# A two-part weight stream in which every other mixing unit gets its low part by an adding transfer

## The chip, the cores and the metric

The kernel runs on one core of a Trainium2 chip. The metric is the device time of one execution in microseconds (us), the median over several runs. The engines are named as in the profile: PE is TensorE (its weight loads are PEld), DVE is VectorE, ACT is ScalarE, POOL is GpSimd, SP is SyncE.

## The reference

The kernel computes a two-layer encoder trunk on a sequence of 512 positions and 1024 channels, in float32. Cut to what matters here, each layer is:

```
h = rmsnorm(x, mix_norm[i])
z = h @ w_in[i]
u_rnn, u_gelu, c_q, ckv_rope, fq, fk, fv, f_logit, gate_logit = split_columns(z)
y_a = rglru_branch(u_rnn, u_gelu, ...) @ w_br_a[i]     # causal conv, gates, associative scan, times GeLU
y_b = mla_branch(c_q, ckv_rope, ...) @ w_br_b[i]       # attention over compressed keys and values
y_c = fox_branch(fq, fk, fv, f_logit, ...) @ w_br_c[i] # attention with cumulative forget gates
g = sigmoid(gate_logit + gate_b[i])
x = x + (g[0] * y_a + g[1] * y_b + g[2] * y_c) @ w_o[i]
x = x + swiglu(rmsnorm(x, ffn_norm[i]))
x = x + sigmoid(rmsnorm(x, ple_norm[i]) @ w_ple_gate[i]) * (p[i] @ w_ple[i])
```

A final RMSNorm follows. Everything up to `w_o` is called the mixing part.

## The kernel before, in words

**Two-part products.** A float32 value is split into a high part (the value cast to the type float32r) and a low part (the value minus the high part). A product of two such values takes three matmuls: high by high, high by low, low by high (`mm3`, whose matmuls are line L237). Activations are kept in pages `pr`, 1024 columns wide: the high part in the first 512, the low part in the rest. Plain float32 pages of 512 columns are `pf` (20 of them).

**The weight stream.** The host packs all weights, in the order of their use, into one DRAM tensor `wst` of 606 units; a unit is 128 partitions by 512 columns of float32, 256 KB, and holds four tiles of 128 columns. Units 0 to 302 belong to layer 0 and 303 to 605 to layer 1; in each layer roughly the first 150 are those of the mixing part. The class `Stream` brings a unit in three steps:

- `_load` (L99) loads it by SP's DMA queue into one of four slots of the tile `raw`.
- `_split` casts it on ACT into the high half of one of eight pages of the tile `hl` (L112), and subtracts on DVE, `raw` minus the high part, into the low half of the page (L113).
- `tile` and `wide` hand the parts to the matmuls. Before a unit u is first used, `_ensure` has written down the splits up to unit u + 7, and the loads up to four units beyond those.

A page of `hl` is free for unit u + 8 when the last matmul of unit u has read it, and a slot of `raw` is free for unit u + 4 when both the cast and the subtraction of unit u have read it. A normal unit feeds 12 matmuls; the four units in `PACKED` feed 8.

**The order of work.** The program is written in the order of the mathematics; the order of the instructions on each engine is then fixed when the kernel is built, by a planner that plays the program through with its own times (`TileContext(nc, schedule_with_timeline_sim=True)`). Instructions under `high_priority()`, which the cast and the subtraction are, go first among those that are ready. On the chip each engine works through its list in that order, and a DMA is issued in the list of the engine that it was given to.

**Around the recurrence.** In `mix` each layer runs in this order: the recurrence's inputs (`ev_u`: convolution on DVE, split into `xcp`), the rotary key and the forget logits (`key_and_forget`, with a chain of small operations on POOL, L376 to L379, a DMA at L527 and one at L534, and a scan on DVE at L537), the GeLU inputs (`ev_ug`), the first pair of keys and queries of the forgetting attention (`fox_proj(0, ...)`, casts at L566), then the gate products of the recurrence (`lru_gate`, four tiles, Tanh and Exp on ACT), then `lru_tail`: four square roots on ACT, and for each of four tiles on DVE two products, a scan (L666), a third product and a split. After it come the values (`values`) and `renorm`, which loads x again through POOL's queue (L695), eight tiles, scales each on DVE, and splits it into the pages `Xn`: the high part by ACT (L233), the low part by DVE. The attention then interleaves its scores with projections (`fp`) and merges (`mg`) that read `X`, `Xn` and the recurrence's result `yA`. The helpers `stt` (L218), `tt` (L221), `ts` (L225 and L227) and `act` (L230) each have one line, so the profile shows much of this under a helper's line. POOL's queue also carries the memsets and small DMAs of the attention heads (L587, L589, L594, L596) and the loads of tables (L495).

Of the kernel before, what the change touches and what calls it, by code (L numbers as in the profile page):

```python
# [10 lines left out]
F32 = mybir.dt.float32  # L11
F32R = mybir.dt.float32r
I32 = mybir.dt.int32
AF = mybir.ActivationFunctionType
ALU = mybir.AluOpType
# [22 lines left out]

NUNITS = 606
KEPT = NUNITS - 16  # L40
PACKED = (8, 9, 311, 312)


# [41 lines left out]
class Stream:  # L85
# [15 lines left out]
    def _split(self, u):  # L101
        s = (u % self.nraw) * 512
        src = self.raw[:, s:s + 512]
        if u >= KEPT:
            self.kept[u] = self.pages.take()
        hi, lo = self._parts(u)
        if u in PACKED:
            hi, lo = (x.rearrange("p (k c) -> p k c", c=128)[:, :, 64 * i:64 * i + 64]
                      for i, x in ((0, hi), (1, hi)))
            src = src.rearrange("p (k c) -> p k c", c=128)[:, :, 0:64]  # L110
        with self.tc.high_priority():
            self.nc.scalar.copy(hi, src)  # L112
            self.nc.vector.tensor_tensor(lo, src, hi.bitcast(F32), op=ALU.subtract)  # L113

    def _parts(self, u, c=slice(0, 512)):
        if u in self.kept:
# [5 lines left out]
    def _ensure(self, u):  # L122
        last = min(u + self.nhl - 1, max(u + 4, KEPT - 1), NUNITS - 1)
        while self.loaded < min(self.nraw, NUNITS):
            self._load(self.loaded)
            self.loaded += 1
        while self.done <= last:
            self._split(self.done)
            self.done += 1
            while self.loaded < min(self.done + self.nraw, NUNITS):  # L130
                self._load(self.loaded)
                self.loaded += 1
# [34 lines left out]
class Trunk:  # L167
# [273 lines left out]
    def mix(self, layer):  # L441
# [69 lines left out]
        def key_and_forget():  # L511
# [3 lines left out]
            for k, x in enumerate(X):  # L515
                assert self.w.pos // 4 in PACKED
                wh, _ = self.w.tile(("kf", L, k))
# [621 lines left out]
    def ple_last(self, X, pw):  # L1139

        L, st = DEPTH - 1, self.st
        self.w.align()
        assert self.w.pos == 4 * KEPT
        fin = [{}, {}]
        half = [slice(0, SEQ // 2), slice(SEQ // 2, SEQ)]

        def part(i, j):
            t = half[i]
            b = self.banks.take()
            for k in range(KD):  # L1150
                if i == 0:
                    wh, wl = self.w.tile(("w_ple_gate", L, 128 * j, 128, k))
                else:
                    wh, wl = self.w.again(4 * KEPT + KD * j + k)
                self.mm3(b[:, :SEQ // 2], wh, wl, X[k].h[:, t], X[k].l[:, t], k == 0, k == KD - 1)
# [236 lines left out]
```

## Time and profile before

| what | value |
|---|---|
| median of 3 runs | 1833.72 us (1833.48 to 1834.23) |
| the profiled execution | 1832.69 us |
| its span, first to last instruction | 1830.8 us |
| granted TensorE clock, mean | 0.992 |
| casts of units on ACT (L112, into `hl`) | 590, 364.2 us busy, 618 ns each |
| subtractions of units on DVE (L113, into `hl`) | 590, 404.6 us busy, 686 ns each |
| read from HBM | 173.98 MB |

The span in 40 equal slices, each digit the busy share of a slice in tenths (9 is 90% or more), PEclk the granted TensorE clock in tenths:

```
PE   9979999999999999999999899999999999999997
DVE  8896678866665555444778966888576655553446
ACT  5755556553333333223448556565533333332243
POOL 1130001100000000000102200010000000000000
PEclk9989999999999999999999999999999999999999
```

PE is full nearly everywhere; the third slice, and the 23rd (the same place in layer 1), are where it is not. The times of single instructions, waits and stretches come from the trace of the same execution; "idle before" or a bracket such as [1.39 <-DVE pr L221] gives how long an engine had been idle before an instruction, and what released it.

### The profile page before, as it was taken

The numbers are of one execution on the slowest core, as the hardware profiler recorded it, in microseconds if no ns is written. First come the engines' busy times: TensorE is split into PE (matmuls) and PEld (weight loads), VectorE is DVE, ScalarE is ACT, GpSimd is POOL, SyncE is SP. The second block draws the span as 40 slices with busy tenths as digits, with TensorE's granted clock in tenths as the row PEclk, the third lists the DMA queues.
The fourth block names the chain that finished last, engine by engine and source line by source line (L and its number), as shares of the span: only waits on it lengthen the run. The fifth ranks groups of instructions, "written<-read, shape, count | busy, mean of one in ns | idle before, by whom it ended". The sixth has DMA issues, their size and how long they took to land.

```text
span 1830.8 us, 24152 instructions
## 1 busy us (share of the span) xinstructions
PE 1805.4 (99%) x8476; PEld 1504.4 (82%) x8476; DVE 1210.4 (66%) x2421; ACT 817.5 (45%) x1562; POOL 117.2 (6%) x234
## 2 busy tenths in 40 slices
PE   9979999999999999999999899999999999999997
PEld 7858888888888888888888788888888888888887
DVE  8896678866665555444778966888576655553446
ACT  5755556553333333223448556565533333332243
POOL 1130001100000000000102200010000000000000
PEclk9989999999999999999999999999999999999999
DMA  6232223324322332322433322243242332233331
GB/s 205 88 117 81 82 81 116 97 71 133 98 93 97 98 98 97 108 95 98 132 111 116 105 85 78 89 121 88 81 131 94 98 97 94 97 110 98 98 98 47
DMA packets 98825, 184.17 MB, mean 101 GB/s; under 512 B 13552, under 2 KB 14752, under 8 KB 98704
## 3 DMA queue, kind: packets, MB, share of 16 engines
q1 hardware_dynamic: 89280, 162.04, 27.1%
q0 software_dynamic: 8416, 19.45, 3.9%
q8 instruction: 66, 1.08, 0.2%
q10 hardware_dynamic: 1008, 1.14, 0.2%
q14 instruction: 55, 0.45, 0.1%
HBM read 173.98 MB, written 4.21 MB: 97 GB/s over the span
## 4 chain that ended last, share of the span: by engine, by line
PE 95%; DVE 3%; ACT 1%; issue 1%; DVEq 0%; ACTq 0%
PE bank L237 93%; PE bank L830 2%; DVE pf L218 1%; DVE pr L221 1%; ACT pf L230 0%; DVE hl L113 0%; DVE pf L666 0%; ACT pr L566 0%; DVE pf L221 0%; DVE pr L218 0%; ACT hl L112 0%; DVE small L838 0%; DVE bank L221 0%; DVE small L218 0%; ACT L230 0%
## 5 line engine op out<-in xcount | busy, mean ns | idle before, releaser
L237 PE MATMUL bank<-pr,hl 128*128 128x512 f32 (+1 forms) x6812 | 1605.2, 392 | 10.6 <-DVE pr L221 5.5
L237 PEld LDWEIGHTS bank<-pr,hl 128*128 128x128 f32 (+1 forms) x6812 | 1269.7, 188 | 274.5 <-DVE pr L221 8.0
L112 ACT CAST hl<-raw 128x512 fp32r<-128x512 f32 x590 | 364.2, 618 | 654.0 <-PE bank L237 438.8
L113 DVE TENSOR_TENSOR hl<-raw,hl 128x512 fp32r<-128x512 f32 x590 | 404.6, 686 | 365.4 <-ACT hl L112 349.5
L221 DVE TENSOR_TENSOR pf<-pf 128x512 f32<-128x512 f32 (+3 forms) x235 | 151.2, 652 | 31.9 <-ACT pf L230 29.8
L221 DVE TENSOR_TENSOR pf<-bank,pf 128x512 f32<-128x512 f32 (+3 forms) x198 | 132.9, 676 | 56.8 <-PE bank L237 31.7
L230 ACT ACTIVATE pf<-pf 128x512 f32<-128x512 f32 (+1 forms) x145 | 86.0, 600 | 112.5 <-DVE pf L221 109.8
L237 PE MATMUL bank<-pr 128*128 128x256 f32 (+4 forms) x704 | 119.6, 301 | 4.1 <-ACT pf L230 4.1
L237 PEld LDWEIGHTS bank<-pr 128*128 128x128 f32 (+1 forms) x704 | 103.9, 191 | 14.5 <-ACT pf L230 4.4
L230 ACT ACTIVATE pf<-bank,small 128x128 f32<-128x128 f32 (+3 forms) x130 | 69.0, 532 | 45.8 <-DVE small L838 42.8
L221 DVE TENSOR_TENSOR pr<-pf,pr 128x512 fp32r<-128x512 f32 (+3 forms) x126 | 85.6, 683 | 4.7 <-ACT pr L233 3.1
L855 ACT CAST pth<-bank 128x128 fp32r<-128x128 f32 (+3 forms) x128 | 54.2, 426 | 69.7 <-PE bank L830 65.6
L233 ACT CAST pr<-pf 128x512 fp32r<-128x512 f32 (+2 forms) x114 | 70.3, 620 | 29.0 <-DVE pf L218 19.2
L838 DVE TENSOR_REDUCE small<-bank 128x1 f32<-128x128 f32 (+3 forms) x128 | 61.7, 485 | 19.2 <-PE bank L237 18.2
L221 DVE TENSOR_TENSOR ptl<-bank,pth 128x128 fp32r<-128x128 f32 (+3 forms) x128 | 61.7, 484 | 13.8 <-ACT pth L855 11.7
L237 PE MATMUL bank<-hl,pr 128*128 128x512 f32 x240 | 56.5, 390 | 0.0
L830 PE MATMUL bank<-identr,pf 128*128 128x128 f32 x320 | 55.4, 274 | 0.0
L237 PEld LDWEIGHTS bank<-hl,pr 128*128 128x128 f32 x240 | 44.9, 188 | 9.2
L225 DVE TENSOR_SCALAR pf<-pf,small 128x128 f32<-128x128 f32 (+3 forms) x128 | 48.3, 383 | 2.6
L218 DVE SCALAR_TENSOR_TENSOR pf<-pf,bank 128x512 f32<-128x512 f32 x48 | 32.7, 684 | 23.7 <-PE bank L237 23.3
L230 ACT ACTIVATE pf<-bank,vec 128x512 f32<-128x512 f32 x60 | 40.9, 689 | 15.1 <-PE bank L237 14.7
L830 PEld LDWEIGHTS bank<-identr,pf 128*128 128x128 f32 x320 | 39.8, 141 | 7.2
(112 smaller groups left out, 793.2 us busy)
## 6 DMA issues: line engine op xcount, KB each, us to landing
raw<-wst SPq DMA_DIRECT2D x606, 256.0 KB, 2.6
pf<-xT POOLq DMA_DIRECT2D x16, 256.0 KB, 3.1
pr<-pr POOLq DMA_DIRECT2D x32, 128.0 KB, 2.5
pf<-xs POOLq DMA_DIRECT2D x16, 256.0 KB, 3.1
pf<-trig POOLq DMA_DIRECT2D x12, 256.0 KB, 3.1
pf<-xT SPq DMA_DIRECT2D x8, 256.0 KB, 5.4
xs<-pf POOLq DMA_DIRECT2D x8, 256.0 KB, 2.8
pf<-pT POOLq DMA_DIRECT2D x4, 256.0 KB, 3.1
```

The costliest lines, as they stand in the source:

```text
L112: self.nc.scalar.copy(hi, src)
L113: self.nc.vector.tensor_tensor(lo, src, hi.bitcast(F32), op=ALU.subtract)
L218: self.nc.vector.scalar_tensor_tensor(out, a, s, b, op0=op0, op1=op1)
L221: self.nc.vector.tensor_tensor(out, a, b, op=op)
L225: self.nc.vector.tensor_scalar(out, a, s1, None, op0=op0)
L230: return self.nc.scalar.activation(out, a, f, **kw)
L233: self.nc.scalar.copy(hi, src)
L237: self.nc.tensor.matmul(out, a, b, start=start, stop=stop, skip_group_check=True)
L830: nc.tensor.transpose(T[:, c], p2.ap[:, c], self.ident[:, :])
L838: nc.vector.reduce_max(R[t][:, 0:1], S[:, :m], axis=AX.X, negate=True)
L855: self.nc.scalar.copy(hi, src)
```

## The change

For 120 units of the mixing part, the odd ones from 11 to 129 in layer 0 and from 315 to 433 in layer 1, the low part is made differently. ACT casts the unit as before (L112). Then ACT, too, writes the negated high part into the low half of the page, and a DMA in POOL's queue reads the same unit a second time from `wst` and adds it to what stands there. DVE's subtraction falls away for these units. The unit is still loaded into `raw` for the cast; that slot is now read by the cast alone. All of it stands under `high_priority()`.

```
+ADDED = {*range(11, 130, 2), *range(315, 434, 2)}
...
         with self.tc.high_priority():
             self.nc.scalar.copy(hi, src)
-            self.nc.vector.tensor_tensor(lo, src, hi.bitcast(F32), op=ALU.subtract)
+            if u in ADDED:
+
+                self.nc.scalar.activation(lo, hi.bitcast(F32), AF.Copy, scale=-1.0)
+                c = 512 * (u % 2)
+                self.nc.gpsimd.dma_start(lo, self.wdram[u // 2][:, c:c + 512], accum_op=ALU.add)
+            else:
+                self.nc.vector.tensor_tensor(lo, src, hi.bitcast(F32), op=ALU.subtract)
```

The order in which the recurrence and the first keys and queries stand is the same before and after. The plan of all engines is made anew for the changed program.

## Prediction

> **What bounds the kernel now.** I read the page first: the busy times and the chain of work that ended last.
>
> ```profile
> PE 1805.4 (99%) x8476; PEld 1504.4 (82%) x8476; DVE 1210.4 (66%) x2421; ACT 817.5 (45%) x1562; POOL 117.2 (6%) x234
> PE 95%; DVE 3%; ACT 1%; issue 1%; DVEq 0%; ACTq 0%
> ```
>
> TensorE (PE) is busy for 1805.4 of 1830.8 us, and 95% of the chain is its own. Taking work off VectorE (DVE) can pay only where DVE is what PE waits for. The 4% of the chain that lies on DVE and ScalarE (ACT) is in two places, one in each layer: around the end of the recurrence, where `lru_tail`, the value evacuations and `renorm` meet. The busy times by stretch show them (columns: stretch, its length, PE, PE weight loads, DVE, ACT, POOL with instruction counts, then granted clock, DMA share, GB/s):
>
> ```profile
> 67.00:90.00 23.00, 23.00 (x104) 19.03 (x103) 16.36 (x29) 22.55 (x37) 8.06 (x18) 1.00 0.31 103
> 90.00:108.00 18.00, 18.00 (x83) 15.01 (x82) 17.91 (x26) 8.88 (x16) 4.74 (x9) 1.00 0.33 104
> 108.00:128.00 20.00, 9.99 (x28) 5.76 (x27) 19.87 (x40) 13.71 (x25) 10.58 (x21) 0.72 0.46 147
> 128.00:132.00 4.00, 4.00 (x14) 3.15 (x13) 4.00 (x10) 1.85 (x5) 0.00 (x0) 0.69 0.16 59
> 972.00:996.00 24.00, 24.00 (x108) 19.88 (x107) 16.08 (x27) 23.75 (x39) 11.21 (x24) 1.00 0.28 88
> 996.00:1020.00 24.00, 24.00 (x110) 19.89 (x109) 24.00 (x39) 14.81 (x26) 8.90 (x18) 1.00 0.49 155
> 1020.00:1028.00 8.00, 3.33 (x11) 1.95 (x10) 7.91 (x15) 5.11 (x11) 3.35 (x7) 0.80 0.34 100
> 1028.00:1032.00 4.00, 4.00 (x11) 3.01 (x11) 4.00 (x11) 1.39 (x3) 0.00 (x0) 0.55 0.32 111
> ```
>
> The same sequence runs in both layers. First ACT is full (22.55 of 23 us; 23.75 of 24) while PE runs on. Then DVE is full for 38 and 32 us, and at the end of that PE starves: it idles 10.0 us in 108 to 128 and 4.7 us in 1020 to 1028, and comes back at a lowered clock (0.69 and 0.55 in the next 4 us). So at most some 15 us of idle time and a few us of slow clock can be won. What ends both stalls, in the timeline of PE:
>
> ```profile
> 127.48 2.93 PE L237 MATMUL bank<-pr,hl 128*128 128x512 f32 x6 [1.39 <-DVE pr L221]
> 1024.57 1.05 PE L237 MATMUL bank<-pr,hl 128*128 128x512 f32 x2 [1.90 <-DVE pr L221]
> 1027.13 5.10 PE L237 MATMUL bank<-pr,hl 128*128 128x512 f32 x12 [1.51 <-DVE pr L221]
> ```
>
> A subtraction that writes a page of split activations (`pr`) releases it, which stands at the end of DVE's queue of work. Every instruction that DVE need not do ahead of it brings PE back earlier.
>
> **Part one: the subtractions that go.** Which units of the stream fall into a stretch comes from counting L113 (and L112) from the start; the n-th is unit n-1:
>
> ```profile
> L113 DVE TENSOR_TENSOR hl<-raw,hl x36: 406/675/730, 6.0 to 85.5; 128x512 fp32r<-128x512 f32 x34, 128x256 fp32r<-128x256 f32 x2
> L113 DVE TENSOR_TENSOR hl<-raw,hl x46: 406/681/730, 6.0 to 123.8; 128x512 fp32r<-128x512 f32 x44, 128x256 fp32r<-128x256 f32 x2
> L113 DVE TENSOR_TENSOR hl<-raw,hl x338: 406/691/730, 6.0 to 991.2; 128x512 fp32r<-128x512 f32 x167, 128x256 fp32r<-128x256 f32 x2
> L113 DVE TENSOR_TENSOR hl<-raw,hl x347: 406/691/730, 6.0 to 1022.6; 128x512 fp32r<-128x512 f32 x172, 128x256 fp32r<-128x256 f32 x2
> ```
>
> These are the counts up to 91.0, 127.4, 995.9 and 1026.9 us. Units 36 to 45 are subtracted in the full stretch of layer 0, units 338 to 346 in that of layer 1. The odd ones are in `ADDED`: five (37 to 45) and four (339 to 345). What one is worth is its pitch, not its duration, since neighbours overlap:
>
> ```profile
> 108.75 0.68 DVE L113 TENSOR_TENSOR hl<-raw,hl 128x512 fp32r<-128x512 f32 x1
> 109.35 0.68 DVE L221 TENSOR_TENSOR pr<-pf,pr 128x512 fp32r<-128x512 f32 x1
> ```
>
> 0.60 us each: 5 x 0.60 = 3.0 us in layer 0 and 4 x 0.60 = 2.4 us in layer 1. The other 111 of the 120 I cost at nothing: PE is busy 99% of the span, and outside the two stalls its own queue of matmuls is the cover. Were that cover gone, each would be worth up to 0.60 us.
>
> **Part two: what ACT gets.** Each added unit costs ACT one more 128x512 instruction, the negation. It doesn't occur in the trace; the nearest rows are the cast with its pitch and the plain activations:
>
> ```profile
> 81.78 0.62 ACT L112 CAST hl<-raw 128x512 fp32r<-128x512 f32 x1
> 82.29 0.83 ACT L230 ACTIVATE pf<-pf,msp 128x512 f32<-128x512 f32 x1
> L230 ACT ACTIVATE pf<-pf 128x512 f32<-128x512 f32 (+1 forms) x145 | 86.0, 600 | 112.5 <-DVE pf L221 109.8
> ```
>
> Between 0.51 us (the cast's pitch) and 0.60 us (the activation's mean); I take 0.55, nearer to the cast, whose types and queue it shares. It matters where ACT is full, before the square roots on which `lru_tail` waits:
>
> ```profile
> L112 ACT CAST hl<-raw x31: 405/622/626, 4.6 to 69.7; 128x512 fp32r<-128x512 f32 x29, 128x256 fp32r<-128x256 f32 x2
> L112 ACT CAST hl<-raw x36: 405/622/626, 4.6 to 84.2; 128x512 fp32r<-128x512 f32 x34, 128x256 fp32r<-128x256 f32 x2
> L112 ACT CAST hl<-raw x332: 405/622/632, 4.6 to 970.8; 128x512 fp32r<-128x512 f32 x164, 128x256 fp32r<-128x256 f32 x2
> L112 ACT CAST hl<-raw x338: 405/622/632, 4.6 to 990.6; 128x512 fp32r<-128x512 f32 x167, 128x256 fp32r<-128x256 f32 x2
> 87.59 1.34 ACT L230 ACTIVATE pf<-pf,eps 128x512 f32<-128x512 f32 x2
> 89.26 1.22 DVE L537 TENSOR_TENSOR_SCAN pf<-one,pf 8x512 f32<-8x512 f32 x1 [3.03 <-DMA pf<-pf]
> 90.50 1.29 DVE L218 SCALAR_TENSOR_TENSOR pf<-pf 128x512 f32<-128x512 f32 x2
> 992.48 1.95 ACT L230 ACTIVATE pf<-pf,eps 128x512 f32<-128x512 f32 x3
> 993.23 1.31 DVE L218 SCALAR_TENSOR_TENSOR pf<-pf 128x512 f32<-128x512 f32 x2 [1.34 <-ACT pf L230]
> ```
>
> The counts are up to 79, 87.5, 974 and 991.1 us: units 31 to 35 and 332 to 337 are cast there, three odd ones each time, so the roots come 3 x 0.55 = 1.65 us later. In layer 1 DVE waits for them (1.34 us, released by ACT), so its full stretch starts 1.65 us later. In layer 0 it doesn't: DVE's tail starts at 90.50, behind the scan of the forget gates, while the first root is done at about 88.3. Shifted by 1.65 that is 89.9, still ahead of 90.50. If the scan itself comes a little earlier, the tail starts 0.5 us earlier; I count those 0.5 us. The scan hangs on a chain of small operations on POOL that starts at 76.46, behind a wait for DVE:
>
> ```profile
> 76.46 0.31 POOL L376 TENSOR_SCALAR pf<-pf 128x32 f32<-128x32 f32 x1 [30.66 <-DVE pf L221]
> ```
>
> Ten subtractions (odd units 11 to 29) are gone from DVE before that point; if only three of them still show there, their 1.8 us pay for the three transfers (units 31 to 35) that now stand in this chain at 0.54 us each.
>
> **Part three: the adding transfers.** Issue and landing of an accumulating transfer aren't in the trace. The nearest are plain 256 KB loads on POOL's queue, one of them issued while DVE is full, and the load on SyncE's queue:
>
> ```profile
> 110.33 0.54 POOL L695 DMA_DIRECT2D pf<-xT  x1 [0.69 <-DVE pr L221]
> pf<-xT POOLq DMA_DIRECT2D x16, 256.0 KB, 3.1
> raw<-wst SPq DMA_DIRECT2D x606, 256.0 KB, 2.6
> q0 software_dynamic: 8416, 19.45, 3.9%
> ```
>
> From below 0.54 us of POOL and 3.1 us to landing; from above twice the landing, 6.2 us, since the old contents have to be read too. I take 4.5 us, between them for want of a nearer row; nothing in the sum depends on it while the lead covers it. The lead is shortest around unit 31:
>
> ```profile
> 79.59 0.61 ACT L112 CAST hl<-raw 128x512 fp32r<-128x512 f32 x1
> 0.00:89.70 89.70, 83.11 (x364) 68.01 (x365) 23.88 (x36) 22.51 (x37) 1.00 0.45 150
> ```
>
> The second row counts instructions on `hl` alone: 364 matmuls are the 31 units 0 to 30 (29 of 12 and two packed ones of 8), so PE reaches unit 31 at 89.70, 10.1 us after its cast began. Cast, negation and transfer take 0.5 + 0.55 + 4.5 = 5.6 us, at most 7.3. Bandwidth is no bound: q0 moved 19.45 MB in 3.9% of the 16 engines' time; 31.5 MB more are 6.3%, or 12.6% if each byte counts twice, on top of 0.46 to 0.49 in the stretches. What the transfer frees is small: an odd unit's `raw` slot comes free after the cast instead of the subtraction.
>
> The Trainium skill, "SBUF — State Buffer", section "SBUF: two separate sides", speaks against the change: while DVE runs an instruction that takes both its ports, GpSimd can't write descriptors, and a 620 ns transfer was seen to take 3100 ns. By it each transfer in a full stretch would, as an estimate, hold POOL about 2.5 us longer, and rival C would be the likeliest. The trace doesn't show it: the load at 110.33 was issued in 0.54 us in a stretch where DVE worked 19.87 of 20 us.
>
> **The sum.** Layer 0: -3.0 - 0.5 = -3.5 us. Layer 1: -2.4 + 1.65 = -0.75 us. Together -4.25 us. The profiled execution took 1832.69 us (span 1830.8 and 1.9 around it), 1.03 us under the median of 1833.72; from 1832.69 it goes to 1828.4, from the median to 1829.5. A change of 0.2%, 3.7 us, is about what a measurement of this kernel can tell from none.
>
> **The rivals.**
> A, the forecast: 1829.5; by itself 1827.8 (without the 1.65 us delay of layer 1's roots) to 1830 (without the 0.5 us).
> B, ACT gives it back: the scan doesn't come earlier, the roots come late in layer 0 too (-3.0 + 1.65 = -1.35), layer 1 as above: -2.1 us, 1831.6. For it: ACT is full ahead of both stretches. Against: the scan, not the roots, opens layer 0's.
> C, slower: POOL's queue becomes the bound. It runs in order (30.66 us of waiting at L376 show it), so an adding transfer whose negation is late holds the `renorm` loads behind it, and Xn comes late.
>
> ```profile
> 119.61 0.56 POOL L695 DMA_DIRECT2D pf<-xT  x1 [2.26 <-DVE pr L221]
> 126.09 0.73 DVE L218 SCALAR_TENSOR_TENSOR pf<-pf,vec 128x512 f32<-128x512 f32 x1
> ```
>
> The last load is issued at 119.61, lands about 122.7 and is used by 126.09 at the latest: 3.4 us of slack. Past that it decides. Five transfers at 0.54 us use 2.7 of it; if each also waits 1 us for ACT (one or two instructions of 0.6), it is 7.7 - 3.4 = +4.3 us, nothing is won by the subtractions, and in layer 1 about the same: +8.6, 1842.3. For it: POOL is busy 10.58 of 20 us there. Against: the casts run far ahead of PE.
> D, more is won: layer 1's stall closes altogether, because DVE's earlier relief (odd units from 315) also reaches ACT. That is 4.7 us idle and 4.0 x (1 - 0.55) = 1.8 us of slow clock; with layer 0's 3.5 us, -10 us, 1823.7. The clock fell to 0.55 after waits of 1.90 and 1.51 us at most.
> The Trainium skill, "TensorE: Matmul & The Clock Gate", section "HAM oscillation — how this bites in real kernels", wants idle gaps over about 3.4 us for that. By its rule the 1.8 us couldn't be lost in layer 1, and D would give 1825.5; the measured clock decides here.
>
> **How the numbers follow.** A 0.42, B 0.25, C 0.21, D 0.12. Faster by over 0.2% (under 1830.1): A and D, 0.54. Within 0.2%: B, 0.25. Slower (over 1837.4): C, 0.21. The range 1823 to 1841 holds A, B and D and the milder part of C; what is left out is C's centre and a transfer that is slow in itself. A's own range is 1827.8 to 1830.
>
> **What would show it right or wrong.** Right: 120 instances of L113 fewer, 120 more ACT instructions of about 0.6 us and 120 transfers of 256 KB on POOL; PE's idle time in layer 0's stretch down from 10.0 to about 6.5 us; layer 1's roots about 1.65 us later against the matmuls. Wrong: PE waiting on a DMA into `hl`; POOL waiting on ACT in front of L695 or the POOL chain of the forget gates; a landing of over 8 us, which would eat unit 31's lead; or an instruction order that differs so much that the stalls lie elsewhere.

## The result and the profile after

The changed kernel takes 1821.28 us (median of 4 runs, 1820.45 to 1821.33), the kernel before 1833.88 us beside it (4 runs, 1833.48 to 1834.23). The ratio is 0.9930, with a 95% interval from 0.9913 to 0.9947: 12.6 us less, where 4.25 were forecast. The direction was right and the size three times too small; the time lies below the range (1823 to 1841).

All lines of the body stand 8 numbers later in the changed kernel: the products are L245, the helpers `stt`, `tt` and `act` L226, L229 and L238. The cast of a unit is L114, the negation L117, the adding transfer L119, the subtraction L121. First the page of the kernel after, whose profiled execution took 1821.33 us: busy times, three groups (line, engine, operation, count; busy us and mean ns; idle time before them) and the queue of POOL's transfers (packets, MB, share of the 16 DMA engines).

```profile
PE 1802.6 (99%) x8476; PEld 1502.5 (83%) x8476; DVE 1140.1 (63%) x2301; ACT 880.4 (48%) x1682; POOL 221.8 (12%) x354
...
q0 software_dynamic: 25696, 50.91, 14.8%
...
L121 DVE TENSOR_TENSOR hl<-raw,hl 128x512 fp32r<-128x512 f32 (+1 forms) x470 | 322.0, 685 | 350.5 <-ACT hl L114 336.2
...
L119 POOL DMA_DIRECT2D hl<-wst x120 | 106.8, 894 | 483.3 <-ACT hl L117 389.6
...
L117 ACT ACTIVATE hl<-hl 128x512 fp32r<-128x512 f32 x120 | 75.7, 631 | 2.0
```

The work moved as the diff says: 120 subtractions fewer, 120 negations and 120 transfers more, DVE 70 us lighter, ACT 63 and POOL 105 us heavier. Hardly any of this shows as time, since PE is busy through nearly all of it. With the span of 1819.6 us, PE's idle time over the whole span went from 1830.8 - 1805.4 = 25.4 to 1819.6 - 1802.6 = 17.0 us, and its busy time fell by 2.8 us for the same 8476 matmuls: less was run at a lowered clock. 8.4 + 2.8 = 11.2 us is the whole difference of the two spans. (It is less than 12.6 because the profiled execution of the kernel before, 1832.69 us, lies 1.2 us under the median beside the change.)

The same stretches as in the prediction, in the kernel after:

```profile
67.00:90.00 23.00, 23.00 (x103) 19.06 (x102) 14.26 (x26) 22.80 (x37) 9.31 (x21) 1.00 0.41 107
90.00:108.00 18.00, 17.94 (x82) 14.65 (x81) 17.94 (x28) 12.40 (x23) 11.10 (x18) 1.00 0.89 219
108.00:128.00 20.00, 15.53 (x56) 11.76 (x55) 19.15 (x42) 14.58 (x30) 9.66 (x19) 0.83 0.61 159
128.00:132.00 4.00, 4.00 (x23) 3.39 (x22) 3.26 (x9) 2.24 (x6) 0.00 (x0) 1.00 0.01 2
972.00:996.00 24.00, 24.00 (x109) 19.88 (x108) 14.86 (x22) 22.80 (x38) 8.88 (x14) 1.00 0.48 114
996.00:1020.00 24.00, 21.73 (x97) 17.30 (x96) 23.90 (x43) 18.39 (x35) 13.59 (x25) 1.00 0.78 220
1020.00:1028.00 8.00, 8.00 (x38) 6.60 (x37) 6.58 (x18) 5.26 (x13) 2.00 (x3) 1.00 0.82 176
1028.00:1032.00 4.00, 4.00 (x24) 3.39 (x23) 1.69 (x4) 1.62 (x4) 0.86 (x1) 1.00 0.81 172
```

In layer 0 PE's idle time fell from 10.0 to 4.5 us (20 - 15.53 and the 0.06 of the row above). In layer 1 it fell from 4.7 to 2.3 us (24 - 21.73), it lies earlier, and the clock no longer drops behind it: 1.00 in 1028 to 1032, where it was 0.55. These 7.9 us are nearly all of the 8.4. So the stalls are where the prediction looked; what ends and opens them, in the timelines of the kernel after:

```profile
118.12 10.03 PE L245 MATMUL bank<-pr,hl 128*128 128x512 f32 x31 [1.94 <-DVE pr L229]
1018.99 0.33 PE L838 MATMUL bank<-identr,pf 128*128 128x128 f32 x1 [1.77 <-DVE pf L233]
1019.58 5.74 PE L245 MATMUL bank<-pr,hl 128*128 128x512 f32 x24 [0.26 <-DVE pr L229]
```

```profile
84.84 1.22 DVE L545 TENSOR_TENSOR_SCAN pf<-one,pf 8x512 f32<-8x512 f32 x1 [2.86 <-DMA pf<-pf]
87.73 1.31 DVE L226 SCALAR_TENSOR_TENSOR pf<-pf 128x512 f32<-128x512 f32 x2 [0.95 <-ACT pf L238]
986.34 1.31 DVE L226 SCALAR_TENSOR_TENSOR pf<-pf 128x512 f32<-128x512 f32 x2 [2.07 <-ACT pf L238]
```

In both layers PE's last waits still end with DVE; the two ahead of them in layer 0 (1.80 and 0.74 us) end with ACT. But the recurrence's tail on DVE starts earlier: in layer 0 at 87.73 instead of 90.50. The scan of the forget gates, behind which it stood, came 4.4 us earlier (84.84 for 89.26), and the tail now waits for the roots. The roots are not 1.65 us late. How far the roots and the tail stand against PE's own work is seen by counting PE's matmuls on `hl` from the start up to each of them (columns: stretch, length, busy time and count, clock, DMA share, GB/s). The kernel before, to its first root and to its tail, and the kernel after, the same:

```profile
0.00:87.59 87.59, 81.00 (x355) 1.00 0.45 151
0.00:90.50 90.50, 83.91 (x368) 1.00 0.45 148
```

```profile
0.00:86.97 86.97, 80.24 (x351) 1.00 0.65 180
0.00:87.73 87.73, 81.00 (x354) 1.00 0.65 180
```

At 81.00/355 = 0.23 us a matmul, the roots come 4 matmuls or 0.9 us earlier, and the tail 14 matmuls or 3.2 us earlier. The length of layer 0's full stretch, from the tail to PE's return, went from 127.48 - 90.50 = 36.98 to 118.12 - 87.73 = 30.39 us; that of layer 1 only from 1027.13 - 993.23 = 33.90 to 1018.99 - 986.34 = 32.65 us.

### The profile page after: what moved, and what is told of

The parts are those of the page before. It is cut to its first block, busy times and chain, and to the rows that moved or that the text cites. A ratio compares the mean times of both kernels' runs of the same rounds, so it can differ in the third digit from the quotient of the medians.

```text
span 1819.6 us, 24284 instructions
## 1 busy us (share of the span) xinstructions
PE 1802.6 (99%) x8476; PEld 1502.5 (83%) x8476; DVE 1140.1 (63%) x2301; ACT 880.4 (48%) x1682; POOL 221.8 (12%) x354
## 3 DMA queue, kind: packets, MB, share of 16 engines
q0 software_dynamic: 25696, 50.91, 14.8%
q8 instruction: 66, 1.08, 0.2%
## 4 chain that ended last, share of the span: by engine, by line
PE 94%; DVE 3%; issue 1%; ACT 1%; DMA 0%; POOL 0%; DVEq 0%; POOLq 0%; ACTq 0%
PE bank L245 92%; PE bank L838 2%; DVE pf L226 1%; DVE pr L229 1%; ACT pf L238 1%; DVE pf L674 0%; DMA pf<-xs 0%; DVE pf L229 0%; DVE pr L226 0%; ACT pr L574 0%; DVE hl L121 0%; POOL pr L597 0%; ACT hl L114 0%; POOL hl L119 0%; DVE small L226 0%
## 5 line engine op out<-in xcount | busy, mean ns | idle before, releaser
L245 PE MATMUL bank<-pr,hl 128*128 128x512 f32 (+1 forms) x6812 | 1602.2, 392 | 3.3 <-DVE pr L229 2.2
L245 PEld LDWEIGHTS bank<-pr,hl 128*128 128x128 f32 (+1 forms) x6812 | 1268.1, 188 | 264.9 <-DVE pr L229 2.7
L114 ACT CAST hl<-raw 128x512 fp32r<-128x512 f32 x590 | 364.0, 618 | 624.8 <-PE bank L245 420.7
L121 DVE TENSOR_TENSOR hl<-raw,hl 128x512 fp32r<-128x512 f32 (+1 forms) x470 | 322.0, 685 | 350.5 <-ACT hl L114 336.2
L229 DVE TENSOR_TENSOR pf<-bank,pf 128x512 f32<-128x512 f32 (+3 forms) x198 | 132.8, 676 | 65.6 <-PE bank L245 33.2
L229 DVE TENSOR_TENSOR pf<-pf 128x512 f32<-128x512 f32 (+3 forms) x235 | 151.1, 652 | 31.7 <-ACT pf L238 29.4
L119 POOL DMA_DIRECT2D hl<-wst x120 | 106.8, 894 | 483.3 <-ACT hl L117 389.6
L238 ACT ACTIVATE pf<-pf 128x512 f32<-128x512 f32 (+1 forms) x145 | 85.7, 600 | 113.7 <-DVE pf L229 110.1
L245 PE MATMUL bank<-pr 128*128 128x256 f32 (+4 forms) x704 | 120.1, 301 | 1.8 <-ACT pf L238 1.8
L245 PEld LDWEIGHTS bank<-pr 128*128 128x128 f32 (+1 forms) x704 | 104.2, 190 | 12.4 <-ACT pf L238 2.1
L229 DVE TENSOR_TENSOR pr<-pf,pr 128x512 fp32r<-128x512 f32 (+2 forms) x126 | 85.5, 682 | 7.3 <-ACT pr L241 4.9
L238 ACT ACTIVATE pf<-bank,small 128x384 f32<-128x384 f32 (+3 forms) x130 | 68.8, 531 | 33.9 <-DVE small L846 30.5
L229 DVE TENSOR_TENSOR ptl<-bank,pth 128x128 fp32r<-128x128 f32 (+3 forms) x128 | 61.8, 485 | 35.3 <-ACT pth L863 26.8
L846 DVE TENSOR_REDUCE small<-bank 128x1 f32<-128x384 f32 (+3 forms) x128 | 61.7, 485 | 24.1 <-PE bank L245 23.1
L241 ACT CAST pr<-pf 128x512 fp32r<-128x512 f32 (+1 forms) x114 | 69.8, 618 | 14.6 <-DVE pf L229 6.6
L117 ACT ACTIVATE hl<-hl 128x512 fp32r<-128x512 f32 x120 | 75.7, 631 | 2.0
L245 PE MATMUL bank<-hl,pr 128*128 128x512 f32 x240 | 56.0, 390 | 0.0
L245 PEld LDWEIGHTS bank<-hl,pr 128*128 128x128 f32 x240 | 44.9, 188 | 9.3
L233 DVE TENSOR_SCALAR pf<-pf,small 128x384 f32<-128x384 f32 (+3 forms) x128 | 49.0, 384 | 3.3
```

Source lines behind the costliest of these rows:

```text
L117: self.nc.scalar.activation(lo, hi.bitcast(F32), AF.Copy, scale=-1.0)
L119: self.nc.gpsimd.dma_start(lo, self.wdram[u // 2][:, c:c + 512], accum_op=ALU.add)
L229: self.nc.vector.tensor_tensor(out, a, b, op=op)
L233: self.nc.vector.tensor_scalar(out, a, s1, None, op0=op0)
L238: return self.nc.scalar.activation(out, a, f, **kw)
L245: self.nc.tensor.matmul(out, a, b, start=start, stop=stop, skip_group_check=True)
```

## The experiments

Each kernel was timed in 3 rounds beside the kernel before, whose median in the four sessions was 1834.17, 1834.59, 1833.83 and 1833.81 us. "Against before" is the difference of the two medians of the same session. The letters of theories are explained in the text of each expectation.

**Which units pay.** Six kernels are the changed kernel with another set of units.

```
early:   ADDED = {*range(11, 37, 2), *range(315, 339, 2)}
stretch: ADDED = {*range(37, 47, 2), *range(339, 349, 2)}
first:   ADDED = {*range(11, 31, 2), *range(315, 333, 2)}
roots:   ADDED = {31, 33, 35, 333, 335, 337}
late:    ADDED = {*range(47, 130, 2), *range(349, 434, 2)}
near:    ADDED = {*range(11, 48, 2), *range(315, 350, 2)}
```

`early` holds the units that are split before DVE's full stretches, `stretch` those in them, `first` and `roots` divide `early`, `late` holds all behind, and `near` the rest together with 47 and 349, which `late` has too.

early: 

> Only the odd units ahead of the two full stretches of DVE get the adding transfer (11 to 35 and 315 to 337), 25 of 120. Theory R (relief ahead of the stretch lets the forget-gate chain and the roots come earlier, so the stretch starts earlier; relief inside it shortens it) expects 3 to 6 us off the 1833.9 of before: the tail starts about 2.8 us earlier in layer 0, and in layer 1 the roots are no later against the matmuls. Theory P (the order that the planner made anew is the gain, whichever units are chosen) expects either next to nothing or nearly all 12.6 us, with no tie to the start of the tail.

stretch: 

> Only the odd units that DVE subtracted inside its full stretches (37 to 45 and 339 to 347), 10 of 120. Theory R expects 0.6 us per subtraction that is gone before PE resumes, five in layer 0 and four or five in layer 1, with no later roots: 5 to 7 us off, a little of it by a shorter time at the lowered clock. Theory P expects no such tie: under 2 us or over 10.

first: 

> Only the odd units ahead of ACT's full stretches: 11 to 29 and 315 to 331, 19 of 120. Theory S expects at least the gain of the 25 early units (10 us off), since the six that burden ACT ahead of the roots are left out: 9 to 13 us off. If the early gain came from the six in ACT's stretch, under 4 us.

roots: 

> Only the odd units that ACT casts in its full stretches, right ahead of the square roots, get the adding transfer: 31, 33, 35 and 333, 335, 337. The prediction's second part, alone: three negations of 0.55 us put the roots 1.65 us later in both layers; in layer 1 the tail of the recurrence starts 1.65 us later against the matmuls. Theory S (ACT's delay is real, but in the whole change it is paid by work that ACT gets done earlier, because DVE feeds it earlier) expects just that here, where nothing feeds ACT earlier: 0.5 to 3 us slower than before. If the negations cost ACT nothing even here, the time stays within 0.5 us.

late: 

> Only the odd units 47 to 129 and 349 to 433 (85 units), those behind the stretches. Theory T: nothing, 1833 to 1836 (within 0.1% of the kernel before). Rival V: 1826 to 1830.

near: 

> Only the odd units 11 to 47 and 315 to 349 (37 of the 120): those ahead of the two full stretches of DVE and in them. Theory T: the whole gain lies here, since outside the stretches PE's own queue covers DVE: 1820 to 1824. Rival V (the units behind the stretches pay too, by some 0.1 us each on 83 units, or by other traffic): 1826 to 1830.

| kernel | units | median us | against before | ratio, 95% interval |
|---|---|---|---|---|
| early | 25 | 1824.04 | -10.1 | 0.9946, 0.9930 to 0.9963 |
| stretch | 10 | 1828.56 | -5.6 | 0.9969, 0.9958 to 0.9980 |
| first | 19 | 1828.46 | -6.1 | 0.9970, 0.9959 to 0.9981 |
| roots | 6 | 1833.82 | -0.8 | 0.9998, 0.9989 to 1.0008 |
| late | 85 | 1834.34 | +0.5 | 1.0003, 0.9994 to 1.0012 |
| near | 37 | 1820.54 | -13.3 | 0.9927, 0.9912 to 0.9942 |

The 37 units ahead of and in the two stretches give the whole gain, and the 85 behind them give nothing. Units in the stretches give about what the prediction worked out for them: -3.0 - 2.4 = -5.4 us forecast, 5.6 measured (the interval reaches from 3.7 to 7.7 us, and the kernel has one unit more than the sum, 347). In `stretch` the tail and PE's return in layer 0, and then in layer 1, are:

```profile
91.58 1.29 DVE L226 SCALAR_TENSOR_TENSOR pf<-pf 128x512 f32<-128x512 f32 x2
```

```profile
125.54 2.93 PE L245 MATMUL bank<-pr,hl 128*128 128x512 f32 x6 [1.47 <-DVE pr L229]
```

```profile
991.90 1.30 DVE L226 SCALAR_TENSOR_TENSOR pf<-pf 128x512 f32<-128x512 f32 x2 [1.35 <-ACT pf L238]
```

```profile
1023.99 2.80 PE L245 MATMUL bank<-pr,hl 128*128 128x512 f32 x6 [3.46 <-DVE pr L229]
```

The stretch of layer 0 lasts 33.96 us, 3.02 less than before: five subtractions at 0.60. That of layer 1 lasts 32.09 us, 1.81 less than the 33.90 of before, though DVE does five subtractions fewer in it as well.

What the prediction missed is in `early`: 10.1 us, from units that it had given -0.5 us in layer 0 and +1.65 in layer 1. The expectations before the runs missed here too: `early` gave more than the 3 to 6 us expected, `first` less than the 9 to 13, and `roots` did not lose the 0.5 to 3. `first` alone gives 6.1 us and `roots` alone nothing that could be measured. In layer 0 `roots` does show the delay that was forecast. Up to its first root PE has done

```profile
0.00:89.66 89.66, 82.53 (x362) 1.00 0.46 152
```

362 matmuls on `hl` instead of 355: 7 x 0.23 = 1.6 us later, where 1.65 was worked out. In layer 1, where alone the sum charged it, the first root (at 994.33) comes after 3965 matmuls instead of 3962: 0.7 us. The parts do not add up. `first` and `roots` give 6.9 us, but `early`, which is both, 10.1; `early` and `stretch` give 15.7, but `near`, which is both and the units 47 and 349, 13.3. Each plan places DVE's other work anew, and what that is worth in each kernel was not separated.

The even units in place of the odd ones:

```
-ADDED = {*range(11, 130, 2), *range(315, 434, 2)}
+ADDED = {*range(12, 131, 2), *range(316, 435, 2)}
```

> The even units from 12 to 130 and 316 to 434 instead of the odd ones: as many subtractions gone in every stretch, but another program for the planner. Theory R expects 10 to 14 us off, as with the odd ones. Theory P expects a time that differs from that of the odd ones by more than 4 us.

1822.07 us, 12.1 less than before (0.9936, 0.9921 to 0.9951). So the gain does not hang on a lucky choice of units or on the one plan that came with them.

**What the added work costs.** Two kernels leave out a part of the low half's computation: `noadd` has no transfer, so that the low part is only the negated high part; `plain` has no negation and a transfer that does not add, so that the low part is the whole weight.

```
 noadd:
-                self.nc.gpsimd.dma_start(lo, self.wdram[u // 2][:, c:c + 512], accum_op=ALU.add)
 plain:
-                self.nc.scalar.activation(lo, hi.bitcast(F32), AF.Copy, scale=-1.0)
-                self.nc.gpsimd.dma_start(lo, self.wdram[u // 2][:, c:c + 512], accum_op=ALU.add)
+                self.nc.gpsimd.dma_start(lo, self.wdram[u // 2][:, c:c + 512])
```

noadd: 

> The change without its transfers: ACT writes the negated high part, nothing is added to it (this leaves part of the computation out). If the 120 transfers cost time (by POOL's queue, by the DMA engines or by late low parts), it is faster than the change by what they cost; the prediction held them for hidden: within 1 us of the change, 1820 to 1822.5.

plain: 

> The change without its negations: the transfer on POOL's queue writes the weights into the low half without adding (this leaves part of the computation out). It takes 120 instructions of 0.55 us from ACT and the reading back from the DMA. Theory S: three of them stand ahead of the roots in each layer, so up to 1.65 us per layer: 1 to 4 us faster than the change. If ACT's share is paid by idle time throughout: within 1 us of it.

`noadd` takes 1821.89 us (-12.7; 0.9936, 0.9922 to 0.9951), `plain` 1822.81 (-11.8; 0.9939, 0.9923 to 0.9956). Both are the change's time within the intervals: neither the transfers nor the negations cost the kernel anything that can be measured, and `plain` is not the 1 to 4 us faster that one theory expected. If POOL's queue were the bound (rival C), `noadd` would be faster than the change.

**DVE's time, the plan, or the slots of `raw`.** `dummy` is the change, and DVE does a subtraction of the same size for each added unit as well, into the unit's slot of `raw`:

```
+                self.nc.vector.tensor_tensor(src, src, hi.bitcast(F32), op=ALU.subtract)
```

> The change as it is, but DVE does a subtraction of the same size for each added unit all the same (into the slot of raw, which nobody reads after it). DVE has its old load back, ACT and POOL keep the new one. Theory R expects the gain to be gone: 0 to 4 us over before. Theory P expects much of the gain to stay, 6 us off or more.

1835.21 us, 1.0 more than before (1.0008, 0.9999 to 1.0017): the gain is gone. But this subtraction also holds the slot of `raw` as long as the old one did, and with an earlier free slot the loads could run further ahead. So `slot` gives DVE other work of much the same size that does not touch `raw`: the maximum of the high part, into a spare column.

```
+        self.w.scr = pool.tile([128, 1], F32, name="scr")
...
+                self.nc.vector.tensor_reduce(self.scr, hi.bitcast(F32), op=ALU.max, axis=AX.X)
```

> The whole change, and for each of the 120 units DVE also takes the maximum of the high part (128x512, into one column of a spare tile) in place of the subtraction that went. DVE's time goes back to about what it was (120 x some 0.6 us), but the raw slot is now freed by the cast alone, as in the change; the kernel with the subtraction put back in place on raw held the slot as before and so couldn't tell the two. Theory T (what pays is DVE's time): the gain is gone, 1832 to 1836. Rival U (what pays is that a slot of raw comes free sooner, so that loads and casts run ahead): the gain stays, 1821 to 1824. Halves of each would stand between, about 1828.

1871.28 us (1.0206, 1.0191 to 1.0221). Neither theory had room for that: PE was slower from the first weight to the last. The spare tile had been put between `hl` and the pages `pr`, and moved the pages. So it was done again with the tile behind all others, and the cause was tried by itself: `shift` is the kernel before with the unused tile between `hl` and `pr`.

slotlast: 

> The kernel with the maximum on DVE again, but with the spare tile as the last tile of SBUF, so that no other tile is moved by it. The first form stood behind the tile hl, moved all later tiles by its 4 bytes per partition, and PE was 3% slower from the start to the end of it, in the feed-forward parts too, where nothing else had changed. Theory T (DVE's time pays): 1832 to 1836. Rival U (the earlier free slot of raw pays): 1821 to 1824. If the tile's place isn't what slowed PE: about 1870 again.

shift: 

> The kernel before, with a tile of one float32 per partition put between hl and the pages pr, and never used: all tiles behind it move. If the place of the activations' pages is what slowed PE by 3% in the first form of the kernel with the maximum: 1880 to 1890. If it was something else in that kernel: 1833 to 1835.

`slotlast` takes 1834.15 us (1.0001, 0.9991 to 1.0010). With the slot free early and DVE's time back, the gain is gone: it is DVE's time that pays, and the earlier slots give nothing that can be measured. `shift` takes 1872.42 us (1.0209, 1.0194 to 1.0225), 38.6 more than before, somewhat less than expected: the place of the tile is what had slowed PE.

How DVE's time reaches the tail is read from the stretch ahead of it, in which no stall is seen. 38 to 67 and 67 to 77 us, in the kernel before, the kernel after, and `slotlast` (PE, weight loads, DVE, ACT, POOL, clock, DMA share, GB/s):

```profile
38.00:67.00 29.00, 29.00 (x129) 24.02 (x129) 27.16 (x49) 16.51 (x29) 0.63 (x1) 1.00 0.26 85
67.00:77.00 10.00, 10.00 (x46) 8.29 (x45) 9.57 (x18) 9.61 (x16) 0.45 (x2) 1.00 0.30 103
```

```profile
38.00:67.00 29.00, 29.00 (x129) 24.03 (x128) 27.05 (x49) 20.74 (x36) 4.91 (x6) 1.00 0.65 153
67.00:77.00 10.00, 10.00 (x46) 8.28 (x45) 7.65 (x15) 9.85 (x18) 4.16 (x9) 1.00 0.39 107
```

```profile
38.00:67.00 29.00, 29.00 (x130) 24.01 (x129) 28.94 (x57) 19.97 (x36) 5.87 (x7) 1.00 0.68 162
67.00:77.00 10.00, 10.00 (x46) 8.29 (x45) 9.88 (x19) 9.55 (x17) 0.85 (x1) 1.00 0.43 116
```

Before, DVE is busy 27.16 of 29 us already here, and ACT, which works on what DVE evacuates, has 12.5 us of idle time. In the change DVE does the same 49 instructions, of which fewer are subtractions, so it is further along (five subtractions instead of eleven). ACT does 36 instead of 29: five of the seven are its own negations, and two are casts of the first keys and queries. The first keys and queries, four casts on ACT, come 5.4 us earlier. Before, and after:

```profile
71.50 2.41 ACT L566 CAST pr<-pf 64x512 fp32r<-64x512 f32 x4
```

```profile
66.14 2.41 ACT L574 CAST pr<-pf 64x512 fp32r<-64x512 f32 x4
```

The chain on POOL that leads to the forget gates' scan starts 3.4 us earlier too:

```profile
73.07 0.30 POOL L384 TENSOR_SCALAR pf<-pf 128x32 f32<-128x32 f32 x1 [2.69 <-DVE pf L229]
```

In `slotlast`, with DVE full again (28.94 of 29, 9.88 of 10), ACT's added negations lie in its idle time as well (19.97 us), but nothing starts earlier (the first casts at 72.71, the chain on POOL at 77.73), and the kernel's time is that of before. The other plans agree. In the eight kernels in which DVE is spared every other unit ahead of the stretches (the change, `even`, `early`, `first`, `near`, `nearfull`, `noadd`, `plain`) these four casts begin between 65.3 and 67.1 us; in the six in which it keeps its time there (the kernel before, `roots`, `stretch`, `late`, `dummy`, `slotlast`) they begin between 71.5 and 72.8 us. So the earlier start is not the luck of one plan.

**Is more to be had?** Two kernels give DVE still less to do. `densefirst` takes every unit, not every other one, of those ahead and in the stretches; `nearfull` only in the stretches.

```
densefirst: ADDED = {*range(11, 48), *range(313, 350)}
nearfull:   ADDED = {*range(11, 36, 2), *range(36, 48), *range(315, 336, 2), *range(336, 350)}
```

densefirst: 

> Every unit (odd and even) from 11 to 47 and from 313 to 349, 74 units, none behind. Theory T, as long as DVE is what the stretches wait for: the idle time of PE left in the change (4.5 us in layer 0, 2.3 us in layer 1) goes too, and the slow clock behind it: 1811 to 1817. Rival W (with twice the negations ACT, which was busy 20.7 of 29 us ahead of the roots, or the DMA engines, whose share stood at 1.0 to 1.1 in 100 to 108 us, are the next bound): 1820 to 1828.

nearfull: 

> The odd units ahead of DVE's full stretches (11 to 35, 315 to 335), and in the stretches every unit (36 to 47, 336 to 349). Theory T, as long as DVE bounds the stretches: four or five more subtractions of 0.6 us go in each, 2 to 5 us less than the change: 1816 to 1820. Rival W (in the stretches ACT is the next bound, as the every-unit kernel's single DVE waits of 4.4 and 5.7 us for ACT suggest): no gain or a loss against the change, 1821 to 1827.

`densefirst` takes 1825.29 us (0.9953, 0.9936 to 0.9970), 8.5 less than before and 4.8 more than `near` in the same session. In it the tails of the two layers wait for the roots:

```profile
87.72 1.31 DVE L226 SCALAR_TENSOR_TENSOR pf<-pf 128x512 f32<-128x512 f32 x2 [4.43 <-ACT pf L238]
```

```profile
987.23 0.69 DVE L226 SCALAR_TENSOR_TENSOR pf<-pf 128x512 f32<-128x512 f32 x1 [5.73 <-ACT pf L238]
```

4.43 and 5.73 us of DVE standing idle: with twice the negations ACT opens the stretch, and the further relief of DVE ahead does not bring the tail of layer 0 forward (87.72, as in the change). This is not the whole loss. In the chain of work that ends at PE's return in layer 0, at 119.05, DVE waits for a load of x:

```profile
116.39 0.75 DVE L226 SCALAR_TENSOR_TENSOR pf<-pf,vec 128x512 f32<-128x512 f32 x1 [0.21 <-DMA pf<-xT]
```

In that chain the load stands for 10.4 us, from 105.98 on, at a DMA share of 0.98; such loads landed in 3.1 us at the median in the kernel before and in 5.0 here. PE also waits 1.8 us in all for transfers into `hl`. How the loss divides between ACT and the DMA engines was not separated.

`nearfull`, which gives ACT no more negations ahead of the roots than the change does, takes 1818.98 us (0.9918, 0.9901 to 0.9934), 14.8 less than before: the fastest kernel of this study. Its stretches show what comes next:

```profile
108.00:128.00 20.00, 17.65 (x70) 13.24 (x70) 18.89 (x45) 16.14 (x35) 12.59 (x23) 0.91 1.01 255
...
996.00:1020.00 24.00, 22.26 (x98) 17.54 (x97) 21.84 (x41) 20.13 (x40) 15.47 (x27) 1.00 1.08 276
```

```profile
1000.77 3.90 PE L245 MATMUL bank<-pr,hl 128*128 128x512 f32 x16 [1.08 <-DMA hl<-wst]
```

The DMA engines are busy throughout (shares 1.01 and 1.08), and PE waits for adding transfers, which it does not in the change: 0.30 us in layer 0, and 1.08 us in layer 1, its longest wait there. The DMA engines are the likely next bound. Against the change the gain is 2.3 us between runs of different sessions, and the intervals overlap; whether it is real is not settled.

## Why the prediction was partly right, and where it failed

**The bound was right.** The time came from PE's stalls around the end of the recurrence: 37 units give all, 85 units nothing, and DVE's time put back takes all away. The reading of layer 0's stall was too short, though. PE's last wait there ends with DVE, but in the kernel before 7.7 of the 10.0 idle us end with ACT, and the longest wait is this:

```profile
119.58 1.22 PE L237 MATMUL bank<-pr 128*128 128x512 f32 x2 [4.07 <-ACT pf L230]
```

ACT in turn waits for DVE there (9.1 us for L218 between 100 and 132 us), and from 110.54 on the chain of work that ends at PE's return at 127.48 is DVE's alone. So DVE is the bound all the same.

**Part one was about right for the stretches** (5.4 us forecast, 5.6 measured by themselves), and wrong in the sentence "The other 111 of the 120 I cost at nothing: PE is busy 99% of the span, and outside the two stalls its own queue of matmuls is the cover." For the units behind the stretches that held (`late`, +0.5 us). For those ahead it failed. PE's queue covers DVE from PE, but it does not cover DVE from ACT and POOL, and their chain opens the stretch. The subtractions of units 11 to 29 stood ahead of layer 0's tail, where DVE was 94% busy (27.16 of 29 us) and fed that chain; with those of layer 1, 315 to 331, they alone are worth 6.1 us (`first`).

**Part two failed with it.** The negation was sized well (0.63 us, at a pitch close to the estimate of 0.55), and the delay of the roots is real when those units alone are changed, but it is 1.6 us in layer 0, where the sum had nothing for it, and 0.7 us in layer 1, where it had 1.65. In the change the relief of DVE lets ACT take up its own work earlier (the first casts 5.4 us), and the five negations from 38 to 67 us fall into ACT's idle time, so in layer 0 the roots come 0.9 us earlier instead of 1.65 later. In layer 1 they also come no later: PE has done

```profile
0.00:992.48 992.48, 929.96 (x3962) 739.05 (x3963) 231.16 (x338) 208.41 (x338) 0.99 0.33 104
```

```profile
0.00:985.58 985.58, 928.87 (x3960) 738.66 (x3961) 181.62 (x266) 250.86 (x407) 62.27 (x70) 1.00 0.45 124
```

3962 matmuls on `hl` up to the first root before, 3960 after. By these rows the kernel after is 6.9 us ahead at that point, less 0.5 us for the two matmuls: of the 11.2 us between the two spans about 6.4 come from layer 0 and about 4.8 from layer 1, where the sum had 3.5 and 0.75. For layer 0's start "I count those 0.5 us" was a guess: ten subtractions go, only three were allowed to show, and 1.8 us less three transfers at 0.54 us is 0.2 us, not 0.5. Measured, the tail starts 14 matmuls or 3.2 us earlier. The terms for these units were the ones most wrongly sized: for the units of `early` the sum had -0.5 + 1.65 = +1.15 us, and they give -10.1.

**What follows from an earlier start was missing.** With it the stretch of layer 0 is 6.6 us shorter, not 3.0. Six subtractions of 0.60 explain 3.6 of it. The rest is other DVE work (51 instructions instead of 64 between the tail and PE's return, six of these thirteen being subtractions), splits and evacuations that the new plan puts elsewhere. How much of that is the relief and how much the plan's luck was not separated; `even`, another set with its own plan, comes out at -12.1. In layer 1 the stretch is only 1.25 us shorter, but PE runs 138 matmuls in it instead of 129; its idle time is halved, and the clock does not fall behind it. Why PE has more to run there was not followed up. Rival D had the mechanism ("DVE's earlier relief ... also reaches ACT") and counted the slow clock that is gone, but at a chance of only 0.12 and for layer 1 alone, and the stall did not close, as D said it would: 2.3 us of it stay.

**Part three was right.** The transfers land in 4.2 us at the median (4.5 taken; 3.6 to 8.6) and hide behind the lead, and the 31.5 MB more cost 14.8 - 3.9 = 10.9% of the DMA engines, between the two bounds. In the kernel after PE waits for no transfer into `hl`, not even where a landing takes over 8 us, which the prediction had named as a sign of being wrong. None of the three transfers of units 31 to 35 stands in the POOL chain. Their issue was under-priced: 0.89 us against 0.54, which cost nothing that `noadd` shows. The hold of 2.5 us that the prediction weighed doesn't come about: in 996 to 1020, with DVE busy 23.90 of 24 us, an adding transfer is issued in 0.90 us, near the mean of all:

```profile
1002.81 0.90 POOL L119 DMA_DIRECT2D hl<-wst  x1 [1.01 <-ACT hl L117]
```

The Trainium skill, "SBUF — State Buffer", section "Who interferes with whom", has the narrower rule that the prediction should have used: a `tensor_tensor` with both inputs in SBUF takes only the read side of the shared ports, as the page infers, and wasn't seen to stall a transfer. The trace agrees, by the 0.90 us above: most of DVE's instructions in that stretch have two inputs (L121, L226, L229).

B and C did not come about. The late roots that B feared are seen where DVE is not relieved ahead of them. In `roots` the tail of layer 0 waits 2.07 us for them, at 90.42; but PE has then done 365 matmuls on `hl` against 368 before, so nothing is lost by it. In `slotlast`, where DVE has its time back and ACT keeps the negations, the roots come after 362 matmuls instead of 355, but the tail follows the scan, which is late too, and starts when PE has done 374, 6 later than before:

```profile
0.00:93.11 93.11, 85.32 (x374) 1.00 0.65 181
```

A trace of C is in layer 1 of the kernel after: one of the `renorm` loads takes 5.7 us to land, beside the adding transfers, and DVE waits 0.68 us for it at 995.97. `noadd`, without the transfers, is not faster, so the kernel's time does not hang on it.

## What to carry to other kernels

An engine that is nearly full ahead of a stall may feed the chain that opens it, though the engine that bounds the kernel sees no wait there: follow the chain of the stall's first instruction back through every engine, and price relief at each place where the relieved engine is close to full. Moving work pays only until the receiver, or the transfers that come with it, set the pace: every other unit gave 13.3 us, every unit 8.5. And when a spare tile is added for an experiment, put it behind all others, or the experiment measures the shift.

## What was not expected of the hardware

**A tile of one float32 per partition ahead of the operands slowed PE by 3%.** In the feed-forward part of layer 0, where PE is full and the clock 1.00, the kernel before and then `shift`:

```profile
560.00:880.00 320.00, 320.00 (x1418) 265.14 (x1417) 158.41 (x252) 100.84 (x170) 3.15 (x6) 1.00 0.31 99
```

```profile
560.00:880.00 320.00, 320.00 (x1373) 257.07 (x1372) 156.08 (x236) 95.48 (x162) 3.15 (x6) 1.00 0.29 96
```

1373 matmuls in 320 us instead of 1418: 233 ns each instead of 226. That it is the address of the operands is the likely reading; by how much the tiles moved, and which offset matters, was not tried. The Trainium skill, "SBUF — State Buffer", section "Door 1: The DMA port swizzle (why `[64,N]` ≈ `[32,N]`)", says that SBUF is read in lines of 16 bytes; pages that no longer begin on such a line would fit, but no run here shows it.

**The clock falls after short waits.** In layer 0 of the kernel after, the longest wait of PE is 1.94 us, and yet (112 to 116, 116 to 120 and 120 to 124 us):

```profile
112.00:116.00 4.00, 1.46 (x5) 0.58 (x4) 3.94 (x7) 3.97 (x9) 3.48 (x7) 1.00 0.85 223
116.00:120.00 4.00, 2.06 (x6) 1.49 (x6) 4.00 (x10) 4.00 (x9) 3.53 (x7) 0.64 0.91 186
120.00:124.00 4.00, 4.00 (x11) 3.13 (x10) 4.00 (x12) 0.82 (x2) 0.55 (x2) 0.51 0.37 89
```

Three such waits in a row (1.80, 0.74 and 1.94 us), 4.5 us idle out of 8, took the clock to 0.51. The Trainium skill, "TensorE: Matmul & The Clock Gate", section "HAM oscillation — how this bites in real kernels", puts the gaps that matter at over about 3.4 us; no single gap here is that long, so the measured clock disagrees with it if a gap means one wait. The sum of the idle time does not settle it either. In `nearfull` two waits of 0.88 and 1.16 us, 2.04 us idle out of 4, are followed by 0.59:

```profile
116.00:120.00 4.00, 1.96 (x7) 0.71 (x5) 3.02 (x11) 4.00 (x11) 4.00 (x9) 0.98 1.08 308
120.00:124.00 4.00, 4.00 (x14) 3.20 (x13) 4.00 (x10) 2.97 (x7) 2.28 (x4) 0.59 1.11 260
```

In layer 1 of the kernel after, from 1016 to 1020 us, PE idles 2.03 us out of 4 (a wait of 1.77 us and a short one behind it), and the clock stays at 1.00. What decides is not shown.

**An adding transfer takes longer than a plain load, and so do the loads beside it.** It takes 0.89 us to issue and 4.2 us to land at the median. The plain 256 KB loads of x on the same queue (`pf<-xT`) took 0.54 to 0.59 us to issue; they landed in 3.1 us at the median before, in 3.8 us in the kernel after, and in 3.4 us in `noadd`, which has no adding transfer.
